# Both parts of the products' weights start 112 bytes later in their tile: one encoder block on one Trainium2 core

## The chip, the cores and the metric

The kernel runs on one core of one Trainium2 chip. The metric is the device time of one execution in microseconds. The median of three runs of the kernel before is 955.25 us (954.86 to 955.66). A profiled execution gives a trace: the start and the length of every instruction on TensorE (the matmul engine; its weight loads are a row of their own), VectorE, ScalarE, GpSimd (called POOL) and of every transfer.

## The reference, cut to what matters

One layer of an encoder on 256 tokens of width 2048, all in float32:

```python
h = rmsnorm(x); proj = h @ w_in                     # q, k, v, u
a = rmsnorm(window_attention(q, k, v, sink)); f = rmsnorm(fourier_mix(u, w_fourier))
x = x + concat([a, f]) @ w_out
h = rmsnorm(x); up = h @ w_up                       # gate and value, 5504 columns each
act = gelu(conv3(gate) + dw_b) * value
x = x + act @ w_down                                # the down projection, 5504 rows
y = rmsnorm(x)
```

The change lies in `act @ w_down`.

## The kernel before, in words

**Two parts for every float32 operand.** TensorE streams a rounded 32-bit type at full rate. To keep float32 accuracy the kernel splits each operand into a rounded first part (`hi`) and the rest (`lo`), and replaces a product by three: first times first, rest times first, first times rest. Weights come from memory in units of 128 x 2048 float32 (1 MB), each into a `raw` tile or, for the down projection, into a `rawd` tile. ScalarE copies the unit into `hi` with rounding, and VectorE subtracts `hi` from the raw unit into `lo`. Both parts lie in one tile called `parts`, of 4224 elements in each partition, with three buffers in turn: `hi` first, `lo` 2048 elements on, and 128 elements to spare. A table, `PLACES`, says by how many elements each of the two starts later than that. It has an entry for four uses: `still` (the unit is the stationary operand of the matmuls: input projection of q and k, and the up projection), `first` and `moving` (the unit is streamed: u and v, and the output projection with the late rows of the down projection), and `product`.

**The down projection by seven products.** For the first 32 row tiles of `w_down` (four groups of eight, `g` = 0 to 3) the kernel multiplies 2 x 2 blocks by a scheme with seven products in place of eight. Its products are named P1, P2, P6, P7, N3, N4 and N5. Four of them take a weight block as it is; three take a sum of blocks, which VectorE and adding transfers of the POOL queue build up in a tile called `sumw`. The activations' side, called `op_P1` and so on, is split by the same rule and is the stationary operand. For each group and each half `c` of the columns all seven are done, so there are 4 x 2 x 7 = 56 products. Each one splits one block (`split_product`, lines 915 and 916) and runs 12 matmuls of 512 columns (`by_parts`, lines 1019 to 1021): over four row tiles, `op`'s first part times `hi`, its second part times `hi`, its first part times `lo`. So `hi` is streamed twice and `lo` once.

**The order.** There is no scheduler: the order on each engine is written out. `PATTERN` mixes the seven products of each half with the gate and value tiles of the next group, product and tile in turn. A gate or value tile (`still_weights`, lines 326 and 328) is 16 pairs of matmuls: one of 512 columns with the weights' first part, and one of 256 columns with their second part. While TensorE works on item n, ScalarE and VectorE do the vector work of earlier items and then the split of item n + 2 (`ff_step`, `split_item`). Three buffers of `parts` make that lead possible. The raw unit's place in the ring is loaded again by the SyncE queue when the split has read it; the adding transfers into `sumw` are issued on the POOL queue after the split that has read the old sum.

Of the kernel before, what the change touches and what calls it, by code (L numbers as in the profile page):

```python
# [83 lines left out]
def block_kernel(  # L84
# [48 lines left out]
    raws, halves = {}, {}  # L133


    PLACES = {"still": (0, 16), "first": (16, 16), "moving": (0, 0), "product": (0, 0)}

    def parts_tile(name, place):
        t = wp.tile([P, 2 * 2048 + 128], F32R, tag="parts", name=name, bufs=3)
        oh, ol = PLACES[place]  # L140
        return t[:, oh : oh + 2048], t[:, 2048 + ol : 4096 + ol]

    def load(i, pieces=1):
        if i < len(units) and i not in raws:
            src, n, _ = units[i]
            raws[i] = wp.tile([P, 2048], F32, tag="raw", name=f"raw{i}", bufs=RAW)
            m = n // pieces
            for p in range(pieces):
                s = slice(p * m, (p + 1) * m)
                nc.sync.dma_start(raws[i][:, s], src[:, s])  # L150
                yield
# [50 lines left out]
    first = load(0, 4)  # L202
# [1082 lines left out]
```

## Time and profile before

| what | value |
|---|---|
| median of three runs | 955.25 us (954.86 to 955.66) |
| the profiled execution's own time | 955.46 us |
| its span, first to last instruction | 953.7 us |
| mean granted TensorE clock | 0.997 of full |
| TensorE busy / weight loads busy | 943.7 us / 813.7 us |
| VectorE busy / ScalarE busy | 745.2 us / 540.4 us |

The profiled execution is 0.21 us above the median, and 1.76 us of it lie outside the span. How to read it: busy time of an engine is the union of its instructions' records. Matmuls are pipelined, and a matmul's record lasts longer than the distance to the start of the next one, so lengths of matmul records are not their cost; the distance between starts is. The chain is the work that ended last, followed back from the last instruction, and its pieces have such distances as their lengths. Instructions are named by line of the kernel, engine, operation and tiles (written tile, an arrow, read tiles), with buffer numbers left out. The products and the tiles between them lie between 365 and 853 us of the span.

### The profile page before, as it was taken

The page shows a single profiled execution, that of the slowest core. Times are in us where ns is not written, and L with a number is a line of the kernel's source. Part 1 is how long each engine was busy: PE and PEld are TensorE (multiplying, and loading weights), DVE is VectorE, ACT ScalarE, POOL GpSimd, SP SyncE. Part 2 cuts the span into 40 slices and gives each one's busy share as a digit, 9 for nine tenths or more (in the row PEclk, how much of TensorE's full clock was granted, in tenths as well). Part 3 has the DMA queues.
Part 4 walks back from the last instruction along what each step waited for, and adds up shares of the span by engine and source line. Part 5 has one row for each costly group of instructions (what it writes and reads, how often), then busy time and mean ns, then how long its engine had stood idle before and what let it go on. Part 6 is the DMA issues. An engine that isn't in the chain of part 4 may idle for free.

```text
span 953.7 us, 12801 instructions
## 1 busy us (share of the span) xinstructions
PE 943.7 (99%) x5089; PEld 813.7 (85%) x5089; DVE 745.2 (78%) x924; ACT 540.4 (57%) x654; POOL 44.6 (5%) x59
## 2 busy tenths in 40 slices
PE   9999999999999999999999999999999999999996
PEld 7788999888888888888888888888888888888885
DVE  5667877666677679887898877988889979888774
ACT  5847666544464456655655555565556755653534
POOL 0000000000000000000000000000000000000003
PEclk9999999999999999999999999999999999999998
DMA  8944444455545675978787787777977696765532
GB/s 309 351 177 177 153 157 144 166 177 179 189 179 218 255 249 189 274 252 268 223 263 235 238 291 252 256 236 221 293 255 244 210 289 204 241 240 204 199 133 89
DMA packets 33548, 211.59 MB, mean 222 GB/s; under 512 B 3792, under 2 KB 4304, under 8 KB 9424
## 3 DMA queue, kind: packets, MB, share of 16 engines
q1 hardware_dynamic: 29744, 184.54, 52.0%
q0 software_dynamic: 3600, 26.22, 14.2%
q8 instruction: 40, 0.66, 0.3%
q14 instruction: 20, 0.16, 0.1%
q10 hardware_dynamic: 144, 0.01, 0.0%
HBM read 208.65 MB, written 2.10 MB: 221 GB/s over the span
## 4 chain that ended last, share of the span: by engine, by line
PE 95%; DMA 2%; DVE 1%; ACT 1%; issue 0%; SPq 0%; POOL 0%; ACTq 0%; POOLq 0%
PE ps_gate L326 16%; PE ps_val L326 16%; PE ps_val L328 8%; PE ps_gate L328 8%; PE ps_q L326 5%; PE ps_P L1020 3%; PE ps_P L1019 3%; PE ps_P L1021 3%; PE ps_q L328 2%; PE ps_a L311 2%; PE ps_a L309 2%; PE ps_a L310 2%; PE ps_N L1019 2%; PE ps_N L1020 2%; PE ps_N L1021 2%; DMA raw<-in_w_in 2%
## 5 line engine op out<-in xcount | busy, mean ns | idle before, releaser
L171 DVE TENSOR_TENSOR parts<-raw,parts 128x2048 fp32r<-128x2048 f32 (+3 forms) x145 | 313.2, 2160 | 62.8 <-ACT parts L170 62.8
L170 ACT ACTIVATE parts<-raw 128x2048 fp32r<-128x2048 f32 (+3 forms) x144 | 262.1, 1820 | 73.9 <-PE ps_l L311 26.0
L326 PE MATMUL ps_val<-hU,parts 128*128 128x512 f32 x688 | 236.8, 390 | 0.0
L326 PE MATMUL ps_gate<-hU,parts 128*128 128x512 f32 x688 | 236.4, 390 | 0.0
L328 PE MATMUL ps_val<-hU,parts 128*128 128x256 f32 x688 | 190.4, 277 | 0.0
L328 PE MATMUL ps_gate<-hU,parts 128*128 128x256 f32 x688 | 189.8, 277 | 0.0
L326 PEld LDWEIGHTS ps_val<-hU,parts 128*128 128x128 f32 x688 | 129.1, 188 | 27.1
L326 PEld LDWEIGHTS ps_gate<-hU,parts 128*128 128x128 f32 x688 | 129.0, 188 | 27.1
L328 PEld LDWEIGHTS ps_val<-hU,parts 128*128 128x128 f32 x688 | 129.2, 188 | 1.2
L328 PEld LDWEIGHTS ps_gate<-hU,parts 128*128 128x128 f32 x688 | 129.0, 188 | 1.2
L810 ACT ACTIVATE ft_g<-ps_gate 128x256 f32<-128x256 f32 x43 | 16.5, 383 | 117.6 <-PE ps_gate L328 117.6
L810 ACT ACTIVATE ft_v<-ps_val 128x256 f32<-128x256 f32 x43 | 16.5, 384 | 90.1 <-PE ps_val L328 90.1
L326 PE MATMUL ps_q<-hT,parts 128*128 128x512 f32 x192 | 61.3, 393 | 0.0
L1020 PE MATMUL ps_P<-parts_P,op_P 128*128 128x512 f32 x128 | 50.2, 392 | 0.0
L1019 PE MATMUL ps_P<-parts_P,op_P 128*128 128x512 f32 x128 | 50.2, 392 | 0.0
L1021 PE MATMUL ps_P<-parts_P,op_P 128*128 128x512 f32 x128 | 49.8, 389 | 0.0
L328 PE MATMUL ps_q<-hT,parts 128*128 128x256 f32 x192 | 45.6, 278 | 0.0
L916 DVE TENSOR_TENSOR parts_N<-sumw,parts_N 128x2048 fp32r<-128x2048 f32 x16 | 36.6, 2290 | 10.1 <-ACT parts_N L915 10.1
L326 PEld LDWEIGHTS ps_q<-hT,parts 128*128 128x128 f32 x192 | 35.2, 188 | 6.8
L309 PE MATMUL ps_a<-parts,cat 128*128 128x512 f32 x96 | 37.9, 395 | 0.0
L1020 PE MATMUL ps_N<-parts_N,op_N 128*128 128x512 f32 x96 | 37.7, 392 | 0.0
L1019 PE MATMUL ps_N<-parts_N,op_N 128*128 128x512 f32 x96 | 37.6, 392 | 0.0
(323 smaller groups left out, 1566.2 us busy)
## 6 DMA issues: line engine op xcount, KB each, us to landing
raw<-in_w_up SPq DMA_DIRECT2D x86, 1024.0 KB, 5.1
raw<-in_w_in SPq DMA_DIRECT2D x21, 1024.0 KB, 5.0
raw<-in_w_out SPq DMA_DIRECT2D x16, 1024.0 KB, 4.8
sumw<-in_w_down POOLq DMA_DIRECT2D x16, 1024.0 KB, 8.4
raw<-in_w_down_late SPq DMA_DIRECT2D x8, 1024.0 KB, 4.8
raw<-in_w_down_last SPq DMA_DIRECT2D x4, 768.0 KB, 4.1
raw<-in_w_in SPq DMA_DIRECT2D x8, 256.0 KB, 7.0
xs<-in_x SPq DMA_DIRECT2D x4, 512.0 KB, 10.7
```

The costliest lines, as they stand in the source:

```text
L170: nc.scalar.activation(hi[:, s], raw[:, s], AF.Copy)
L171: nc.vector.tensor_tensor(lo[:, s], raw[:, s], f32(hi[:, s]), ALU.subtract)
L309: nc.tensor.matmul(ps, ah, wh, start=first and q == q0, stop=False)
L310: nc.tensor.matmul(ps, al, wh, start=False, stop=False)
L311: nc.tensor.matmul(ps, ah, wl, start=False, stop=last and q == q0 + len(kk) - 1)
L326: nc.tensor.matmul(ps, hi[:, s], h, start=k == 0, stop=False)
L328: nc.tensor.matmul(ps[:, 0:S], lo[:, s], h[:, 0:S], start=False, stop=k == NK - 1)
L810: nc.scalar.activation(tmp, ps[:, S : 2 * S], AF.Copy)
L916: nc.vector.tensor_tensor(lo, src, f32(hi), ALU.subtract)
L1019: nc.tensor.matmul(ps, o[:, 0, p, :], hi[:, s], start=first and p == 0, stop=False)
L1020: nc.tensor.matmul(ps, o[:, 1, p, :], hi[:, s], start=False, stop=False)
L1021: nc.tensor.matmul(ps, o[:, 0, p, :], lo[:, s], start=False, stop=last and p == 3)
```

## The change

One pair of numbers in the table changes. Both parts of a product's weight block start 28 elements, 112 bytes, later in the `parts` tile; the tile, its size, its buffers and all other uses of it stay as they are. The two splits of a product write there, the second split reads there, and the product's 12 matmuls stream from there.

```diff
-    PLACES = {"still": (0, 16), "first": (16, 16), "moving": (0, 0), "product": (0, 0)}
+    PLACES = {"still": (0, 16), "first": (16, 16), "moving": (0, 0), "product": (28, 28)}

     def parts_tile(name, place):
         t = wp.tile([P, 2 * 2048 + 128], F32R, tag="parts", name=name, bufs=3)
         oh, ol = PLACES[place]
         return t[:, oh : oh + 2048], t[:, 2048 + ol : 4096 + ol]
```

## The prediction

> **What bounds the kernel now.** I read the page first (busy shares, the 40 slices, the chain), then the busy times of one stage, then the chain in order of time inside that stage.
>
> ```profile
> span 953.7 us, 12801 instructions
> PE 943.7 (99%) x5089; PEld 813.7 (85%) x5089; DVE 745.2 (78%) x924; ACT 540.4 (57%) x654; POOL 44.6 (5%) x59
> PEclk9999999999999999999999999999999999999998
> PE 95%; DMA 2%; DVE 1%; ACT 1%; issue 0%; SPq 0%; POOL 0%; ACTq 0%; POOLq 0%
> ```
>
> TensorE is busy in 99% of the span, and 95% of the chain that ended last is TensorE work at the full granted clock. A view of busy time cannot say whether a busy TensorE is at its quickest, since the records of neighbouring matmuls overlap. The distance from one start to the next says that, and the chain in order of time gives it. One product, between two projection tiles, reads so there (start, length on the chain, operation):
>
> ```profile
> 499.60 0.11 PE ps_val L328
> 499.71 0.23 PE ps_P L1019
> 499.94 0.24 PE ps_P L1020
> 500.18 0.23 PE ps_P L1021
> 500.40 0.23 PE ps_P L1019
> 500.64 0.23 PE ps_P L1020
> 500.87 0.23 PE ps_P L1021
> ...
> 502.23 0.23 PE ps_P L1021
> 502.45 0.23 PE ps_gate L326
> ```
>
> Twelve matmuls of 512 columns stand between 499.71 and 502.45: 2.74 us, 0.2283 us each. The first five take 1.16 us (499.71 to 500.87, 0.232 each), the other seven 1.58 us (0.226 each): there is a short unevenness at the change of pattern and then a steady pitch. Nothing waits in between. How many such matmuls there are, by the source line of the first of the three:
>
> ```profile
> L1019 PE MATMUL ps_P<-parts_P,op_P x128: 388/391/396, 365.6 to 843.7; 128*128 128x512 f32 x128
> L1019 PE MATMUL ps_N<-parts_N,op_N x96: 388/393/401, 382.0 to 851.9; 128*128 128x512 f32 x96
> ```
>
> 128 + 96 = 224 on that line, three lines to a set, so 672 matmuls in 56 products. 56 x 2.74 = 153.4 us, 16% of the span, and all of it on the path: **each nanosecond of pitch is worth 672 x 0.001 = 0.67 us.**
>
> **The change, part by part.** No instruction is added, removed or moved on any engine, no wait and no DMA is new. What moves is the start of two byte ranges. In the built program the three buffers of the parts tile start 93,984, 110,880 and 127,776 bytes into a partition, each 32 bytes past a multiple of 128. Both halves of a product's weights start there too (the second 8192 bytes on). With 112 bytes more they start 16 bytes past a multiple of 128. The products' stationary operands keep starts that are 32 bytes past one. So three users of these ranges see a new start: ScalarE writes the first part, VectorE reads it and writes the second, and TensorE streams both.
>
> *The splits (ScalarE and VectorE).* Rows by line and form: of the splits, first the long ones of the other stages (in most of them the second part already lies 64 bytes further on), then those of the products; last the two neighbour taps of the convolution, which work one element (4 bytes) off from each other. The columns are busy us, mean ns of one, idle time before:
>
> ```profile
> L171 DVE TENSOR_TENSOR parts<-raw,parts 128x2048 fp32r<-128x2048 f32 x130 | 297.5, 2288 | 55.2 <-ACT parts L170 55.2
> L916 DVE TENSOR_TENSOR parts_N<-sumw,parts_N 128x2048 fp32r<-128x2048 f32 x16 | 36.6, 2290 | 10.1 <-ACT parts_N L915 10.1
> L915 ACT ACTIVATE parts_N<-sumw 128x2048 fp32r<-128x2048 f32 x16 | 30.5, 1909 | 0.0
> L824 DVE SCALAR_TENSOR_TENSOR cv<-fa_g,vec,cv 128x255 f32<-128x255 f32 x43 | 20.8, 484 | 1.5
> L821 DVE SCALAR_TENSOR_TENSOR cv<-fa_g,vec,cv 128x255 f32<-128x255 f32 x43 | 20.6, 479 | 0.0
> ```
>
> 64 bytes change a split by 2 ns of 2290, and 4 bytes change a tap by 5 ns of 480. I cost the splits at nothing: bounds 0 and, scaling 5 ns in 480 to the long operation, 24 ns on VectorE; ScalarE shows no row with an odd start, so I give it the same 1%, 20 ns. What hides that is the lead of the splits over the matmuls, and the place where that lead is thinnest:
>
> ```profile
> 502.42 2.28 DVE L916 TENSOR_TENSOR parts_N<-sumw,parts_N 128x2048 fp32r<-128x2048 f32 x1
> ```
>
> ```profile
> 507.75 0.39 PE L1019 MATMUL ps_N<-parts_N,op_N 128*128 128x512 f32 x1
> ```
>
> ```profile
> 806.78 2.29 DVE L916 TENSOR_TENSOR parts_N<-sumw,parts_N 128x2048 fp32r<-128x2048 f32 x1
> ```
>
> ```profile
> 808.77 0.40 PE L1020 MATMUL ps_N<-parts_N,op_N 128*128 128x512 f32 x1
> 809.12 0.50 PE L1021 MATMUL ps_N<-parts_N,op_N 128*128 128x512 f32 x1
> ```
>
> Usually the second part is ready (502.42 + 2.28 = 504.70) three microseconds before its first matmul (two pitches after 507.75). Once, at 809, there is no lead: VectorE ends at 809.07 and TensorE starts at 809.12, 0.35 us after the matmul before. There 24 + 20 ns would be paid, 0.04 us in all. If the cover were gone everywhere, 56 x 0.044 = 2.5 us. Behind a late split stand, on VectorE, the next projection's split and, on the POOL queue, the transfer that adds into the sum tile once the split has read it; both have the same microseconds of lead.
>
> *The matmuls (TensorE).* Here nothing hides a loss, and no row of this trace shows a streamed operand that starts 16 bytes past a multiple of 32: every long one starts 32 or 96 bytes past a multiple of 128. The nearest rows, in order of nearness:
>
> First, a streamed operand with an odd start. The Fourier step streams 129 columns from the start of a tile and 127 from byte 516 of it:
>
> ```profile
> L510 PE MATMUL ps_y<-uf,G 128*128 128x127 f32 x8 | 1.5, 274 | 0.0
> L510 PE MATMUL ps_y<-uf,G 128*128 128x129 f32 x8 | 1.5, 274 | 0.0
> ```
>
> Two columns fewer, and still 274 ns. At the 0.44 ns a column that the 512- and 256-column records differ by ((390 - 277)/256, below), the odd start costs about 1 ns. That is plain f32, not the rounded type of the products, and it is short; per matmul it would be 672 x 0.001 = 0.7 us.
>
> ```profile
> L326 PE MATMUL ps_gate<-hU,parts 128*128 128x512 f32 x688 | 236.4, 390 | 0.0
> L328 PE MATMUL ps_gate<-hU,parts 128*128 128x256 f32 x688 | 189.8, 277 | 0.0
> ```
>
> Second, the same pair of matmuls at two cadences. Two k tiles of the input projection, same code, same phases of the addresses:
>
> ```profile
> 58.22 1.17 PE ps_k L326 x5
> 59.51 0.23 PE ps_k L326
> 59.86 0.23 PE ps_k L326
> ...
> 63.24 0.59 PE ps_k L328 x5
> ```
>
> ```profile
> 111.20 1.14 PE ps_k L326 x5
> ...
> 112.46 0.23 PE ps_k L326
> 112.68 0.11 PE ps_k L328
> 112.80 0.23 PE ps_k L326
> ...
> 116.08 0.59 PE ps_k L328 x5
> ```
>
> The pair of a 512- and a 256-column matmul comes every 0.35 us in one (59.51 to 59.86) and every 0.34 in the other (112.46 to 112.80), and the stretch is 5.02 against 4.88 us: 2.9% more, without a wait. [...] A step of 2.9% on the products is 153.4 x 0.029 = 4.4 us. The upper end comes from the slowest cadence of short matmuls, five in 0.59 us, 0.118 for 256 columns or 0.236 for 512: 672 x (0.236 - 0.2283) = 5.2 us; or two such steps, 8.9 us. Below nothing: the same step taken the other way, -4.4 us, because no row excludes that the new start takes away what makes the pitch.
>
> I take +4.4 us, one step, over the 1 ns of the odd-start row, because the products are of the rounded type at full rate like the k tiles, and the Fourier row is not. Why up and not down: all long matmuls, whether streamed and stationary starts are equal (products) or 64 bytes apart (first part of the projections), hold 0.226 to 0.227 when steady; the trace shows slower cadences in several places and no quicker one, so an unknown shift has more room above. The profiled execution took 955.46 us, 0.21 over the median; the shift is the same on either: 955.25 + 4.4 + 0.04 = **959.7 us**.
>
> **The rivals.**
>
> *Nothing happens.* For it: the pitch is alike at the two phases the trace shows, and the odd-start row gives at most 0.7 us. Against it: 16 bytes past 32 is a phase that no long stream has had. Time: 955.3, up to 956.2. [...]
>
> *Faster: the weight load stops getting in the way.* Streamed and stationary starts are now equal modulo 128, and both are read at once; if their lines meet in the memory and that makes part of the pitch, 16 bytes apart could free it. One step down: 153.4 x 0.971, 950.8 us; it decides once the pitch falls by 3 ns (2 us). For it: weight loads run beside the streams all the time. Against it: 64 bytes apart, in the projections, bought no quicker 512-column pitch. [...]
>
> *Slower through VectorE.* If a start off 32 bytes slows the splits by much, the splits become late, not the streams. Here is the stage:
>
> ```profile
> 490.00:616.00 126.00, 126.00 (x684) 108.94 (x683) 107.39 (x110) 72.90 (x69) 5.24 (x6) 1.00 0.79 250
> ```
>
> The columns are length of the stage, then busy TensorE, weight loads, VectorE, ScalarE. VectorE is busy 107.39 of 126.00 us with 14 products in it, so each split could grow by 18.6/14 = 1.3 us, over half its length, before VectorE is full. Doubled splits (2.3 us more) would add 14 x 1.0 = 14 us a stage, some 50 us over four. I see nothing that points there.
>
> **How the numbers follow.** Slower cadence 0.48 (959.7), nothing 0.27 (955.3), faster 0.23 (950.8), late splits 0.02. What a measurement can tell from no change is 0.2%, 1.9 us. The cases map straight on: faster 0.23, same 0.27, slower 0.50. The range takes one step down (950.8, less the spread of the runs shown) and two steps up (955.3 + 8.9 = 964.2): 950 to 965, which leaves out the late splits, a gain of more than one step and a loss of more than two, under 2 in 10 together. The likeliest case alone: 957.5 to 964.5.
>
> **What would show it.** Right: in the chain, a product's twelve matmuls take 2.80 to 2.85 us instead of 2.74, with no wait before them; the projection tiles between keep 0.34 us a pair; L915 and L916 keep 1909 and 2290 ns. Wrong, no change: 2.74 again. Wrong, faster: 2.65 or less. Wrong by mechanism: L916 above 2.4 us, or idle time of TensorE put down to VectorE in more places than 809.

## The result, and the profile after

| | before | after |
|---|---|---|
| median | 954.81 us (12 executions, 953.94 to 955.66) | 952.71 us (12 executions, 951.26 to 953.34) |
| the profiled execution's own time | 955.46 us | 953.02 us |
| its span | 953.7 us | 951.2 us |

The ratio is 0.9976 with a 95% interval of 0.9967 to 0.9984: the change made the kernel faster by about a quarter of a per cent. I had forecast 959.7 us, slower by half a per cent.

The page after, its head, its busy times and the shares of the chain:

```profile
span 951.2 us, 12801 instructions
PE 940.7 (99%) x5089; PEld 813.0 (85%) x5089; DVE 744.8 (78%) x924; ACT 540.3 (57%) x654; POOL 44.7 (5%) x59
PE 92%; DVE 3%; DMA 2%; issue 1%; ACT 1%; SPq 0%; POOL 0%; ACTq 0%; POOLq 0%
```

The same instructions, still a TensorE that is busy in 99% of the span, 3 us less of it, and VectorE and ScalarE as before. So the time came out of matmuls that were already back to back. The groups by line and form show that the splits, which write and read at the new place, did not get longer (2290 and 1909 ns before):

```profile
L916 DVE TENSOR_TENSOR parts_N<-sumw,parts_N 128x2048 fp32r<-128x2048 f32 x16 | 36.6, 2290 | 10.1 <-ACT parts_N L915 10.1
...
L915 ACT ACTIVATE parts_N<-sumw 128x2048 fp32r<-128x2048 f32 x16 | 30.6, 1910 | 0.0
```

The chain in order of time through one product, which answers to the one shown of before (start, length on the chain, operation):

```profile
498.90 0.11 PE ps_val L328
499.01 0.23 PE ps_P L1019
499.24 0.23 PE ps_P L1020
499.47 0.23 PE ps_P L1021
499.69 0.23 PE ps_P L1019
499.92 0.23 PE ps_P L1020
...
501.51 0.23 PE ps_P L1021
501.74 0.23 PE ps_gate L326
```

Before, two of the first matmuls stood 0.24 us apart; now there is one even pitch from the first to the last. Two decimals are too coarse for the rest, so the trace's starts in nanoseconds, medians over all products: before, the twelve distances begin 231, 235, 228, 233, 231 and go on at 226 to 227; after, all are 226 to 227. One product takes 2745 ns before and 2720 after. The tile behind a product shows the same: before, its pairs begin with 232 and 118, then 227 and 120, then 232 and 113, and settle at 227 and 113; after, they run 227 and 113 from the first pair. It takes 5462 ns before and 5440 after. **What vanished is a short unevenness at each change between product and tile; the steady pitch is what it was.**

A ruler that the page's two decimals can bear is the distance from the first matmul of a group's first product (P1) to that of its last (N4), 13 cycles of a product and a tile later, in the second group. Timeline of TensorE, before:

```profile
491.34 0.39 PE L1019 MATMUL ps_P<-parts_P,op_P 128*128 128x512 f32 x1
...
598.03 0.39 PE L1019 MATMUL ps_N<-parts_N,op_N 128*128 128x512 f32 x1
```

and after:

```profile
490.69 0.39 PE L1019 MATMUL ps_P<-parts_P,op_P 128*128 128x512 f32 x1
...
596.77 0.39 PE L1019 MATMUL ps_N<-parts_N,op_N 128*128 128x512 f32 x1
```

106.69/13 = 8.207 us a cycle before and 106.08/13 = 8.160 after, 47 ns less, which is 25 for the product and 22 for the tile. Over 56 products and the 55 tiles behind them that is 1.40 + 1.21 = 2.6 us. The other stages (u and v, q and k, the output projection, the tiles before the first product) took the same to 0.1 us.

A tenth of a microsecond is given back. In the last group TensorE comes to the second part of product N5 2.33 us earlier than before (the matmul ahead of it, L1020, starts at 806.44 in place of 808.77). VectorE has that part ready only 2.19 us earlier (806.88 in place of 809.07): ahead of the split it does a block of eight sums (L1006 to L1013). VectorE's timeline after:

```profile
798.74 0.69 DVE L1006 TENSOR_TENSOR z_P<-ps_P,z_P 128x512 f32<-128x512 f32 x1
...
803.20 0.68 DVE L1013 TENSOR_TENSOR xs<-xs,sum 128x512 f32<-128x512 f32 x1
804.60 2.28 DVE L916 TENSOR_TENSOR parts_N<-sumw,parts_N 128x2048 fp32r<-128x2048 f32 x1
```

and TensorE's:

```profile
806.21 0.39 PE L1019 MATMUL ps_N<-parts_N,op_N 128*128 128x512 f32 x1
806.44 0.39 PE L1020 MATMUL ps_N<-parts_N,op_N 128*128 128x512 f32 x1
806.93 0.50 PE L1021 MATMUL ps_N<-parts_N,op_N 128*128 128x512 f32 x1
```

VectorE ends at 806.88 and the matmul that waits starts at 806.93, 0.49 us after the one ahead of it, where 0.35 stood before. So the matmuls gained 2.6 us, the longer wait took back 0.14, and the profiled execution shortened by 955.46 - 953.02 = 2.44.

### The profile page after: what moved, and what is told of

Same layout as the page of the kernel before. It is cut to its first block, busy times and chain, and to the rows that moved or that the text cites. A ratio compares the mean times of both kernels' runs of the same rounds, so it can differ in the third digit from the quotient of the medians.

```text
span 951.2 us, 12801 instructions
## 1 busy us (share of the span) xinstructions
PE 940.7 (99%) x5089; PEld 813.0 (85%) x5089; DVE 744.8 (78%) x924; ACT 540.3 (57%) x654; POOL 44.7 (5%) x59
## 4 chain that ended last, share of the span: by engine, by line
PE 92%; DVE 3%; DMA 2%; issue 1%; ACT 1%; SPq 0%; POOL 0%; ACTq 0%; POOLq 0%
PE ps_val L326 16%; PE ps_gate L326 16%; PE ps_val L328 8%; PE ps_gate L328 8%; PE ps_q L326 5%; PE ps_P L1020 3%; PE ps_P L1021 3%; PE ps_P L1019 3%; PE ps_q L328 2%; PE ps_a L311 2%; PE ps_a L309 2%; PE ps_a L310 2%; PE ps_N L1021 2%; PE ps_N L1020 2%; PE ps_N L1019 2%; DMA raw<-in_w_in 2%
## 5 line engine op out<-in xcount | busy, mean ns | idle before, releaser
L1020 PE MATMUL ps_P<-parts_P,op_P 128*128 128x512 f32 x128 | 49.8, 389 | 0.0
L916 DVE TENSOR_TENSOR parts_N<-sumw,parts_N 128x2048 fp32r<-128x2048 f32 x16 | 36.6, 2290 | 10.1 <-ACT parts_N L915 10.1
L309 PE MATMUL ps_a<-parts,cat 128*128 128x512 f32 x96 | 37.9, 394 | 0.0
L1021 PE MATMUL ps_N<-parts_N,op_N 128*128 128x512 f32 x96 | 37.5, 390 | 0.1
L311 PE MATMUL ps_a<-parts,cat 128*128 128x512 f32 x96 | 37.5, 390 | 0.0
```

Of the source, the lines that this page charges most:

```text
L309: nc.tensor.matmul(ps, ah, wh, start=first and q == q0, stop=False)
L311: nc.tensor.matmul(ps, ah, wl, start=False, stop=last and q == q0 + len(kk) - 1)
L916: nc.vector.tensor_tensor(lo, src, f32(hi), ALU.subtract)
L1020: nc.tensor.matmul(ps, o[:, 1, p, :], hi[:, s], start=False, stop=False)
L1021: nc.tensor.matmul(ps, o[:, 0, p, :], lo[:, s], start=False, stop=last and p == 3)
```

## The experiments

In the prediction I had called a slower or a quicker cadence "a step", had taken its size from two k tiles (5.02 against 4.88 us), and had guessed the direction; what picks between two cadences, no row of before shows. The experiments ask what the cadence depends on. Four theories:

- **V**: where the splits write and read (the vector engines, not TensorE).
- **S**: where the streamed operand starts, by itself.
- **R**: only the difference between the streamed and the stationary start.
- **L**: both starts as they are, and what went before them.

"Start" is a byte address in a partition, modulo 256 unless said otherwise. Before, the streams of the products start at 32 and their stationary operands at 32; after the change the streams start at 144. The ruler is the cycle (8.207 before, 8.160 after); the product alone is from the starts in nanoseconds, as above. The times of the kernel before were taken beside each run, on the same chip. All medians and ratios are of whole kernels; all nanoseconds are from one trace of each run.

### One part alone

```diff
-    PLACES = {"still": (0, 16), "first": (16, 16), "moving": (0, 0), "product": (0, 0)}
+    PLACES = {"still": (0, 16), "first": (16, 16), "moving": (0, 0), "product": (28, 32)}
```

> The first part of a product's weights starts 112 bytes later as in the change, the second part 128 bytes later, so that its phase against multiples of 128 bytes is that of before. Theory R (the streamed operand and the weight load read beside it collide when their starts are equal modulo 32 bytes; a collision costs the unevenness of 25 ns at the start of a product and 21 ns at the start of the tile behind it): the first five matmuls of a product hold two streams of the first part, then one of the second, so most of the 25 ns goes; a product 2.72 to 2.73 us, time -1.2 to -2.4 us. Theory V (what counts is where ScalarE and VectorE write, not what TensorE reads): no forecast of its own beyond a difference between this run and the next. Theory S (only the start of the stream itself matters, whatever the weights' start): as R.

Measured: first part at 144, second at 160: 955.2 against 954.25 us, ratio 1.0009 (0.9999 to 1.0018). The product takes 2757 ns, and its pitch does not settle (227, 227, 232, 232, 233, 228, 232, 225, 232, 234, 231, 224).

```diff
+    PLACES = {"still": (0, 16), "first": (16, 16), "moving": (0, 0), "product": (0, 28)}
```

> Only the second part of a product's weights starts 112 bytes later; the first part stays. Theory R and S: the first two matmuls of a product, which pay 4 + 9 of its 25 ns, still collide, so a product takes 2.73 to 2.745 us, and the time falls by 0 to 1.2 us.

Measured: first part at 32, second at 144: 961.13 against 954.25 us, ratio 1.0072 (1.0057 to 1.0087). Here is the slower cadence that I had forecast. TensorE's timeline:

```profile
493.83 0.39 PE L1019 MATMUL ps_P<-parts_P,op_P 128*128 128x512 f32 x1
...
601.97 0.39 PE L1019 MATMUL ps_N<-parts_N,op_N 128*128 128x512 f32 x1
```

108.14/13 = 8.319 us a cycle. The product takes 2781 ns in the median, 231.8 a matmul. More of the loss is in the tiles, whose addresses are those of before. The chain through a tile:

```profile
488.39 0.23 PE ps_gate L326
488.62 0.12 PE ps_gate L328
488.74 0.23 PE ps_gate L326
488.97 0.12 PE ps_gate L328
489.09 0.23 PE ps_gate L326
```

Each pair takes 0.35 us where it took 0.34, through all 16 pairs, at a granted clock of 1.00. This tile follows another tile and not a product (5600 ns here, 5440 in the change), so **the slower cadence stands also in matmuls whose own addresses did not change.** Not every tile is slow: the products take 2768, 2790 and 2780 ns in turn, and the tiles behind them 5599, 5600 and 5443. The turn is not that of the three `parts` buffers. Where two more tiles stand between two products, which shifts the buffers, the next product takes the figure that was due. What follows from both runs: neither part alone does what both do, and the parts' places do not add up.

### How far, and in which grid

The two parts start alike in all of these.

```diff
+    PLACES = {"still": (0, 16), "first": (16, 16), "moving": (0, 0), "product": (4, 4)}
```

> Both parts start 16 bytes later instead of 112, that is 48 past a multiple of 128 bytes: the same half of a 32-byte unit as the change, but the other side of the stationary operand's start. Theory R with 32 bytes: a product 2.720 us, the tile behind it 5.327, time as after the change, 2.3 us under before. If the unit is longer (64 or 128 bytes) and the change hit one lucky place of it: 2.745 us and the time of before.

```diff
+    PLACES = {"still": (0, 16), "first": (16, 16), "moving": (0, 0), "product": (8, 8)}
```

> Both parts start 32 bytes later, 64 past a multiple of 128 bytes. Theory R with a unit of 32 bytes: starts equal again, a product 2.745 us, time of before (0.0 us). With a unit of 64 or 128 bytes: starts differ, 2.720 us and -2.3 us.

```diff
+    PLACES = {"still": (0, 16), "first": (16, 16), "moving": (0, 0), "product": (24, 24)}
```

> Both parts start 96 bytes later, so that every stream starts at a multiple of 128 bytes. Theory R with a unit of 32 bytes: equal starts modulo 32, 2.745 us a product, 0.0 us. [...]

```diff
+    PLACES = {"still": (0, 16), "first": (16, 16), "moving": (0, 0), "product": (60, 60)}
```

> Both parts start 240 bytes later, 128 more than in the change: 16 bytes past a multiple of 256 where the change is 144 past one. What the seven runs so far left standing is theory L: a start of a stream and of a weight load is smooth or not by both addresses, and the cadence is handed on from matmul to matmul, so that a product ends in a steady 0.2267 us a matmul, or never settles. If only the place within 128 bytes counts: products of 2.720 us and 2.3 us under before. If the place within 256 bytes counts (the op tiles of the run with the stationary operands moved, 128 bytes apart from each other, fell into two classes of 2.796 and 2.801 us): another figure, by the products so far between 2.745 and 2.811 us, 0 to 4 us more.

```diff
+    PLACES = {"still": (0, 16), "first": (16, 16), "moving": (0, 0), "product": (92, 92)}
```

> Both parts start 368 bytes later, 256 more than in the change. Theory L with a period of 128 or 256 bytes: the change over again, a product 2.720 us, the tile behind it without a surplus, -2.3 us. With a longer period, or if the 112 bytes acted through something else than the place within a unit: another figure.

```diff
+    PLACES = {"still": (0, 16), "first": (16, 16), "moving": (0, 0), "product": (28, 28)}
```

> The changed kernel once more, to stand beside the two versions of the same call: 2.3 us under before (ratio 0.9976).

| run | streams start at | product, ns | cycle, us | ratio (95%) | median us (before) |
|---|---|---|---|---|---|
| before | 32 | 2745 | 8.207 | | |
| e3, 16 bytes | 48 | 2781 | 8.220 | 1.0008 (0.9999 to 1.0017) | 955.01 (954.25) |
| e4, 32 bytes | 64 | 2794 | 8.233 | 1.0015 (1.0005 to 1.0024) | 955.85 (954.25) |
| e7, 96 bytes | 128 | 2811 | 8.260 | 1.0028 (1.0017 to 1.0039) | 957.44 (954.52) |
| e8, 240 bytes | 16 | 2809 | 8.280 | 1.0038 (1.0023 to 1.0053) | 958.53 (954.96) |
| e9, 368 bytes | 144 | 2720 | 8.160 | 0.9974 (0.9964 to 0.9984) | 952.16 (954.96) |
| e10, 112 bytes, the change once more | 144 | 2720 | 8.160 | 0.9983 (0.9975 to 0.9992) | 952.58 (954.45) |

Timeline rows of TensorE in the two that decide, first e8 (128 bytes further than the change):

```profile
491.75 0.39 PE L1019 MATMUL ps_P<-parts_P,op_P 128*128 128x512 f32 x1
...
599.39 0.39 PE L1019 MATMUL ps_N<-parts_N,op_N 128*128 128x512 f32 x1
```

and e9 (256 bytes further than the change):

```profile
490.19 0.39 PE L1019 MATMUL ps_P<-parts_P,op_P 128*128 128x512 f32 x1
...
596.27 0.39 PE L1019 MATMUL ps_N<-parts_N,op_N 128*128 128x512 f32 x1
```

107.64/13 = 8.280 and 106.08/13 = 8.160. 128 bytes beyond the change the gain has turned into a loss, and 256 bytes beyond it the cycle is the change's to the nanosecond. So a period of 128 bytes is excluded and one of 256 fits, as far as these places show. It is no matter of a round start: e7, at a multiple of 128, is among the slow ones. Of all places tried, 144 alone gives the even pitch. In e3 the product repeats 228, 234, 235, 230 to its end, in e7 and e8 it wanders between 230 and 240. The expectations that R gave for e1 to e4, with unequal starts modulo 32 bytes as the cure, lay between 2.72 and 2.745 us a product, and all were missed: 2757, 2781, 2781 and 2794 ns.

### The stationary side

```diff
-        t = wp.tile([P, 2 * 2048 + 128], F32R, tag="parts", name=name, bufs=3)
+        t = wp.tile([P, 2 * 2048 + 64], F32R, tag="parts", name=name, bufs=3)
...
-        o = fp.tile([P, 2, 4, P], F32R, tag=f"op_{name}", name=f"op_{name}", bufs=1)
+        t = fp.tile([P, 8 * P + 32], F32R, tag=f"op_{name}", name=f"op_{name}", bufs=1)
+        o = t[:, 4 : 4 + 8 * P].rearrange("p (a b c) -> p a b c", a=2, b=4)
```

The first two lines make room in the memory; modulo 256 the places of the streams stay those of before (the second and third buffers move by 256 and 512 bytes). The rest moves the stationary operands 16 bytes on, to 48 (P1, P6, P7, N5) and to 176 (P2, N3, N4).

> The products' weights stay where they are before the change; the stationary operands (the seven op tiles) start 16 bytes later instead, 48 past a multiple of 128 bytes. The split writes and the streams are as before. Theory R (relative starts of stream and weight load): a product 2.720 us and about -2.3 us. Theory S (the start of the stream alone) and theory V (the places that the splits write): 2.745 us and 0.0 us.

The second takes the same edit and moves the streams by 16 bytes as well (`"product": (4, 4)`), so that the difference between the two starts is again that of before:

> Both the products' weights and the stationary operands start 16 bytes later, so that their starts are equal again. Theory R: 2.745 us a product, time of before (0.0 us). Theory S and V: 2.720 us and -2.3 us.

Measured: e5 957.59 against 954.52 us, ratio 1.0030 (1.0019 to 1.0041); e6 959.76 against 954.52, ratio 1.0052 (1.0037 to 1.0067). The timeline of e5, whose kernel is one line longer, so that L1020 is the first of the three:

```profile
491.31 0.40 PE L1020 MATMUL ps_P<-parts_P,op_P 128*128 128x512 f32 x1
...
598.64 0.40 PE L1020 MATMUL ps_N<-parts_N,op_N 128*128 128x512 f32 x1
```

107.33/13 = 8.256 a cycle, the product 2800 ns. But for whole multiples of 256 bytes, the streams and the splits that write them lie where they lay, so **V and S fall**: the place of the stationary operand changes the cadence by itself. The weight loads last 187 to 192 ns in the median of each line, against 188 before. Within e5 the products with a stationary start of 48 take 2801 ns and those of 176 take 2796, so 128 bytes make a small difference on this side too. e6's cycle is 8.298 and its products 2780 to 2800. Its first three (P1, P7, N5) have the difference of before and no product with another one ahead of them; they take 2786 or 2787 ns where that difference gave 2745: **R falls**. L stands, as the one that is left and the widest of the four.

### Is it the change of pattern?

If the surplus belongs to the change between product and tile, half as many changes should have half of it, and the change should gain half as much. Two products and two tiles in turn, once on the kernel before and once with the change:

```diff
-PATTERN = "uuu" + "su" * 13 + "s"
+PATTERN = "uuu" + "ssuu" * 6 + "ssu"
```

> The kernel before with two products in a row and then two tiles, in place of product and tile in turn: the same 56 products and tiles, half the changes of pattern. Theory L (the surplus belongs to the change of pattern and dies out within five matmuls): the first product of a pair takes 2.745 us, the second 2.720; the first tile 5.462, the second 5.440; 28 x 0.046 = 1.3 us less than before in these stretches, whatever waits the new order adds elsewhere. If the surplus belongs to each product (its own starts): 2.745 and 5.462 each time, no gain.

> The changed kernel in the same paired order. Theory L: products 2.720 and tiles 5.440 us as without pairs, so no gain from the pairing; waits that the new order adds come on top. If pairing helps the changed kernel as much, the surplus was not what the change removed.

Measured: 969.11 and 967.94 us against 955.49, ratios 1.0148 (1.0131 to 1.0166) and 1.0132 (1.0115 to 1.0148). The order itself costs some 13 us, since a group's first products now come before their stationary operands are ready. Waits of the weight loads in e14 (us in total, times, longest), within 0.1 us the same in e13:

```profile
PEld ps_P L1020 <- DVE op_P L879: 8.9, 4, 2.2
...
PEld ps_P L1019 <- ACT op_P L878: 2.0, 4, 0.5
```

Behind these waits the granted clock falls to 0.50 for 3.4 us, four times in the trace of e13 and three times in that of e14. The medians differ by 1.2 us, where the four runs of each overlap, so they do not decide. The cadence is read in the first group, clear of those waits, over four times two products and two tiles. e13:

```profile
385.03 0.39 PE L1019 MATMUL ps_N<-parts_N,op_N 128*128 128x512 f32 x1
...
450.49 0.39 PE L1019 MATMUL ps_N<-parts_N,op_N 128*128 128x512 f32 x1
```

e14:

```profile
383.90 0.39 PE L1019 MATMUL ps_N<-parts_N,op_N 128*128 128x512 f32 x1
...
449.18 0.39 PE L1019 MATMUL ps_N<-parts_N,op_N 128*128 128x512 f32 x1
```

65.46/4 = 16.365 and 65.28/4 = 16.320: 45 ns a pair of products, where the kernel before loses 47 with each product. In this stretch of e13 the first product of a pair takes 2745 ns and the second 2720, the first tile 5462 and the second 5440; in e14 all take 2720 and 5440. So **with the addresses of before, the cost stands at the change of pattern**, 25 ns going into a product and 22 going into a tile, and the matmuls find the even pitch again after about five. In the products of e1 to e8 they don't find it.

The last group of e14 shows something that neither the expectation nor the first three groups have. TensorE's timeline there, first matmuls of two pairs of products that follow each other:

```profile
772.00 0.39 PE L1019 MATMUL ps_N<-parts_N,op_N 128*128 128x512 f32 x1
...
788.74 0.39 PE L1019 MATMUL ps_P<-parts_P,op_P 128*128 128x512 f32 x1
```

16.74 us, where the first group has 16.32, with no wait and at a granted clock of 1.00. Eight products in a row take 2773 or 2774 ns each, repeating 225, 231, 237, and the tiles among them take 5600; then the last four take 2720 again. The places of the operands are those of the first group. **So the changed kernel has a slower lasting cadence too, at the same addresses.** The slow stretch begins where the clock comes back to full in the middle of a tile; in the second and third groups it comes back within a product, and the even pitch follows within a few matmuls. Whether that is what decides is not shown.

### A better version, and a second use of the place

The eight sums that VectorE does in one block ahead of N5's split are spread, one for each item, for the first half of the columns. The change is kept.

```diff
-        tt(u, p1, u, ALU.add)
-        tt(x00, p1, x00, ALU.add)
+        tt(u, p1, u, ALU.add)
+        yield
+        tt(x00, p1, x00, ALU.add)
+        yield
...
-                at(behind, n + 1, shared_out, c)
+                steps = shared_out(c)
+                for m in range(9):
+                    at(behind, n + 1 + (m if c == 0 else 0), next, steps, None)
```

> The change, and the eight sums of VectorE behind the last group's first half (lines 1006 to 1013, 5 us in a row) are issued one behind each of eight items in place of all at once. In the changed kernel TensorE waits about 0.37 us at 806 for the second part of product N5 behind those sums. Theory L and the view of VectorE's queue alike: that wait goes, 0.3 to 0.4 us less than the change alone (0.04%). If other splits become late instead, the wait shows up behind later items and nothing is gained.

Measured: 951.6 against 954.45 us, ratio 0.9970 (0.9960 to 0.9981), the best of all; its interval overlaps those of the change, so how much of that is the wait is not shown by the times. The trace shows that the wait is gone (this product took 3139 ns in e10 and takes 2720 here):

```profile
804.86 0.39 PE L1027 MATMUL ps_N<-parts_N,op_N 128*128 128x512 f32 x1
805.09 0.39 PE L1028 MATMUL ps_N<-parts_N,op_N 128*128 128x512 f32 x1
805.32 0.39 PE L1029 MATMUL ps_N<-parts_N,op_N 128*128 128x512 f32 x1
```

These are N5's matmuls in the last group, 0.23 us apart (the kernel is eight lines longer here); all 56 products take 2720 ns.

On top of that, the streams of the output projection and of the late rows of the down projection get the same place (32 bytes to 144):

```diff
-    PLACES = {"still": (0, 16), "first": (16, 16), "moving": (0, 0), "product": (28, 28)}
+    PLACES = {"still": (0, 16), "first": (16, 16), "moving": (28, 28), "product": (28, 28)}
```

> As the run with the sums spread, and the streamed weights of the output projection and of the late rows of the down projection start 112 bytes later too. Their stationary operands start 32 bytes past a multiple of 256 as those of the products do. Theory L: the output projection's 16 units, 87.9 us for 384 matmuls (0.2289 each), lose the surplus that comes behind each group of attention matmuls, at most 16 x 25 ns, 0.4 us; the late units about 8 x 10 ns. If the history (other short matmuls in front) decides and not the addresses alone, they may as well get slower.

Measured: 954.82 against 954.45 us, ratio 1.0002 (0.9993 to 1.0011): the gain of e11 is lost again. The output projection took 89.25 us in place of 87.91, which is less than half of the 3.2 us between the medians of e12 and e11; the products are as even as in e11, and most of the rest is not placed. The chain there, in e12:

```profile
239.25 0.24 PE ps_a L311
239.49 0.23 PE ps_a L309
239.71 0.23 PE ps_a L310
239.94 0.24 PE ps_a L311
240.18 0.23 PE ps_a L309
```

It repeats 225, 231, 238 ns from start to end, 0.69 us for three where the even pitch has 0.68. Later in the same kernel, in the late rows, streams and stationary operands with these same starts run evenly:

```profile
911.87 0.23 PE ps_l L309
912.10 0.23 PE ps_l L310
912.32 0.23 PE ps_l L311
912.55 0.23 PE ps_l L309
...
913.23 0.23 PE ps_l L309
```

0.68 us for three (911.87 to 912.55, and 912.55 to 913.23). The cadence of 225, 231, 238 is the one that the last group of e14 has. So the addresses alone do not fix the cadence: **there are at least two lasting ones for the same starts.** A slower cadence also lasts: in e2 through all 16 pairs of a tile of 5600 ns, in e14 through eight products of 2773 ns in a row. That what ran before decides which one comes is the second half of L. It is how I read these traces; no run changes that alone, and by what it would decide is open.

## Why the prediction was wrong, point by point

- **What bounds the kernel: right.** All of the difference is in how closely matmuls follow each other, and all of that lies on the path, as the prediction had it: the shortened distances, 2.6 us, less the 0.14 of the longer wait, are within 0.02 us the 2.44 by which the profiled execution shortened.
- **The splits at nothing: right.** 1910 and 2290 ns.
- **"There 24 + 20 ns would be paid" at 809: another size, another cause.** The wait there did grow, by 0.14 us, but not through longer splits: TensorE comes 2.33 us earlier and VectorE 2.19. e11 removes it.
- **"I take +4.4 us, one step": the step that failed.** It has two faults. One is that I listed "a short unevenness at the change of pattern" among what the reader should see and then summed only the steady pitch, as if the unevenness were fixed. It was the term: 25 ns in each product and 22 in each tile behind it, 2.6 us, and the change removed all of it. The first five matmuls at 0.232 against 0.226 priced the product's half in my own rows: 5 x 6 ns x 56 = 1.7 us by their two decimals, 1.4 as measured. The tile's half I never looked at, since the change does not touch the tiles. The other fault is that one slower step of the steady pitch, borrowed from two k tiles, was taken for what an unknown start would bring: the pitch is 226.7 ns before and after. The "full rate" of the products is, in the trace of before, those 227 ns for 512 columns from start to start, where four matmuls of plain float32 with 512 columns (`ps_g`, L471) start 428 ns apart and take 1.72 us on the chain.
- **"Why up and not down": refuted as argued, though the odds it stood on were real.** Of the eight other placements of both sides that I tried (e1 to e8), none is quicker and six are slower by more than nothing; e9 repeats the change. An unknown shift did have more room above; only this one was the exception, and I know of nothing in the trace of before that tells it from the others. The size of a step was too large for most, 0.46%: e4, e5, e7 and e8 lose 0.15 to 0.38%, e6 0.52% and e2 0.72%.
- **"The projection tiles between keep 0.34 us a pair": nearly right here, wrong in general.** They do after the change, and lost their uneven start; in e2 two tiles of three run at 0.35 throughout.
- **The faster rival: right in sign, wrong in its mechanism.** It asked for a steady pitch one step down, 2.65 us a product and 950.8. The steady pitch is unchanged, the product is 2.720, and the time is 952.7. Unequal starts are not enough for it either: in e3 they are 16 bytes apart, and the product goes up to 2781 ns.
- **Range and signs: luck.** The 952.7 us lie between 950 and 965 because the range reached down to the faster rival, not because the likeliest case came near. The signs named products of 2.74, 2.80 to 2.85 and 2.65 us; the 2.72 that came stood for none of them.
- **The rival "nothing": refuted here.** It had for it that the pitch is alike at the two starts which the trace of before shows. The steady pitch is alike after the change too, 226.7 ns, and yet the start of the stream reaches the product: it goes from 2745 ns to 2781 with 16 bytes (e3) and to 2720 with 112 (the change). A period of 256 bytes fits the runs.
- **The weight load's part: measured, not explained.** In e5 only the stationary operands lie elsewhere, and the product goes from 2745 to 2800 ns, so the place that the load reads does reach the stream. That the two meet in the memory, as the faster rival had it, is one reading of it, which is argued and not shown: no run here shows lines of the memory, or separates a collision from some other beat between load and stream.

What stays open is the rule. L says what the cadence depends on, as far as these runs go, and not which place is good; 144 was found, not derived. Why a start matters to the cadence at all is open too.

## What to carry to other kernels

Where TensorE is busy nearly all the time and waits for nothing, read the distances between the starts of its matmuls, in nanoseconds, on both sides of every change of operand pattern; a few uneven starts, times the number of changes, are a term of the sum (here 47 ns a cycle, 2.6 us). Moving an operand by some bytes can win or lose that term (here 0.24% won, up to 0.72% lost), so try a few places modulo 256 for each stage, and time the whole kernel each time, because matmuls that were not moved can get slower too (in e2 tiles of 5600 ns, 5440 in the change). A place that was good in one stage was bad in another (144: the product went from 2745 to 2720 ns, the output projection in e12 from 87.91 to 89.25 us), so none is carried over untested.

## What the runs showed of the hardware that I had not expected

- The start of a matmul's operand matters in steps as small as 16 bytes: for twelve matmuls, 2745 ns became 2781 with the streamed operand 16 bytes on (e3) and 2800 with the stationary one (e5). Over all places of the stream it was 2720 to 2811. For the streamed one a period of 256 bytes fits (2720 ns at 144 and at 144 + 256) and one of 128 does not (2809 at 16).
- The same work has more than one lasting cadence. At the same addresses it runs at an even 226.7 ns or repeats 225, 231, 237 (e14, 2720 or 2773 ns a product), and tiles whose addresses did not change run 5440 or 5600 ns (e2), without a wait.
- No place tried made the steady pitch quicker than 226.7 ns for 512 columns; the places only changed how much of the time it was reached.
- The long operations of VectorE and ScalarE took the same wherever they started: the products' splits of the summed blocks take 2289 to 2293 ns on VectorE and 1905 to 1914 on ScalarE at every place of the streams tried.
